# Steps with seven products in a float32 two-block decoder kernel: their number and place set per matrix pair, with buffers of their own

## The chip, the cores and the metric

The kernel runs on one core of one Trainium2 chip. The metric is device time in microseconds for one execution of the whole program. An execution is also taken with the hardware profiler; the traces below are of such executions, and their times (us) count from the first instruction.

## The reference, cut to what matters

Two decoder blocks on 256 tokens of width 2048, all in float32. Nearly all work is `activations (256 x 2048) @ weight (2048 x n)`:

```python
h = rms_norm(x, g)
(qa, ka, va, za, qb, kb, vb, zb, qm, zm, gates) = split(h @ w_in)      # 17408 columns
ya = moba_attention(rope(qa), rope(ka), va) * silu(za)
yb = dilated_mixture(rope(qb), rope(kb), vb) * silu(zb)
ym = memory_attention(qm, mem_n @ w_mem_kv) * silu(zm)
merged = g_a*(ya @ w_proj_a) + g_b*(yb @ w_proj_b) + g_m*(ym @ w_proj_m)
x1 = rms_norm(x + merged @ w_out, norm_final_g)
u = rmsnorm(x1, ln1_w)
lru_x, lru_g, q, k, v, ret_g = split(u @ w_in_2)                       # 6144 columns
y = concat(rg_lru(conv(lru_x)) * gelu(lru_g), retention(q, k, v, ret_g))
h1 = x1 + y @ w_out_2
u2 = rmsnorm(h1, ln2_w)
h2 = h1 + (silu(u2 @ w_ffn_gate) * (u2 @ w_ffn_up)) @ w_ffn_down       # 5632 wide
out = rmsnorm(h2, final_norm_w)
```

## The kernel before

**Splitting.** To reach float32 accuracy each operand is split in a rounded part and a rest (`hi`, `lo`; `split`, L327): ScalarE (ACT) copies to `hi`, VectorE (DVE) subtracts to get `lo`. A product of two 128x128 / 128x512 blocks is then three matmuls: hi·hi, hi·lo, lo·hi (L239 to L241, L179 to L181). The activations are split once (`Lhs`), the weights as they come: a 1 MB tile `raw` (three buffers) is loaded by SP's queue, and from it come `hi`/`lo` tiles of 128x2x512 (four buffers each).

**Single matrices** (`gemm`, L171): 512 output columns, two row tiles of 128 tokens, 16 blocks of 128 along the contraction. Each `hi`/`lo` tile feeds twelve matmuls.

**Pairs** (`pair_gemm`, L224): two matrices of 512 columns at once, in steps of 256 along the contraction. A step of kind "D" makes the plain eight block products (24 matmuls) from two `hi`/`lo` tiles. A step of kind "S" is Winograd's form of Strassen's scheme: seven products (21 matmuls), for which DVE first forms sums of weight blocks, `t13` (L274) and `t24` (L275, L276), and the activations' sums have been made once by `Lhs.put` (L160 to L169). It needs three full `hi`/`lo` tiles and a half one. The seven products go to PSUM banks "1" to "7", those of D steps to "2", "4", "3", "8". After the last S step (index `s1`) banks 1, 6, 7, 5 are combined (L294 to L298) and after the last step banks 2, 4, 3, 8 are added (L299 to L302), into four tiles `p1`, `vv`, `ww`, `yy` of the ring `w512` (eight buffers, L70).

**Which steps are S** stands in the table `STEPS` (L27), one string for each left operand: `lx` (first block's input), `u2` (input of gate/up), `ff` and `ff3` (input of the down matrix; `ff3` for the last three of the eleven 512-wide parts). The order of the steps is the order of the contraction. The matrices and their names in the traces: `qm`, `zm`, `qva`, `kza`, `gate` (three groups), `b` on `lx`; `wo` (both output matrices: `w_out` from L766, `w_out2` from L999); `lx`, `rq`, `rk`, `rv`, `lg`, `rg` (second block's input); `gu` (gate/up, L1037) and `fd` (down, L1054 and L1057). Before, the third gate group (`gate_one`, L644), both `wo` and all of the second block's input are single matrices.

**Side work** (attention, transposes for the next left operand, statistics) is cut into pieces that wait in two queues (`later`, `soon`); a `gemm` takes one up after each of its `hi`/`lo` tiles, a pair after each half of a D step that does not lie between its first and last S step (L290). `need` takes up pieces at once until a key is done.

**The order on each engine** is made by a scheduler from the program: it places instructions by its own estimate of time and gives a tile a buffer of its ring when one is free; each engine then runs its row in that order and waits on semaphores. 27 general buffers of 4 KB per partition (`slot`, L66) hold activations and results. The softmax tiles and `t13`, `t24` share two rings of two ("prob", "pt").

Of the kernel before, what the change touches and what calls it, by code (L numbers as in the profile page):

```python
# [13 lines left out]
ALU = mybir.AluOpType  # L14
# [37 lines left out]
def two_blocks(ctx: ExitStack, tc: tile.TileContext, x, xT, mem, memT, w_in, w_mem_kv, w_proj_a,  # L52
# [6 lines left out]
    sp = ctx.enter_context(tc.tile_pool(name="sp", bufs=NSLOT))  # L59
# [9 lines left out]
    def w512(name, shape=(P, 512)):  # L69
        return tp.tile(list(shape), F32, tag="w512", name=name, bufs=8)  # L70
# [52 lines left out]
    class Lhs:  # L123
# [24 lines left out]
        def put(self, i, src, gains=None, gain=None):  # L148
# [11 lines left out]
            a = tp.tile([P, 8, P], F32, tag="pt", name="fa")  # L160
# [10 lines left out]
    def gemm(name, w, r0, nk, col0, lhs, fine=False, tail=False, rate=1):  # L171
# [52 lines left out]
    def pair_gemm(name, wa, ca, wb, cb, lhs, r0=0):  # L224
        kinds = lhs.kinds
        n = len(kinds)
        s0, s1 = kinds.index("S"), kinds.rindex("S")
# [26 lines left out]
        for i, kind in enumerate(kinds):  # L254
            raw = wp.tile([P, 4, 512], F32, tag="raw", name="raw", bufs=3)
# [11 lines left out]
            if kind == "S":  # L267
# [35 lines left out]
        return (p1, w), (y, v)  # L303

# [183 lines left out]
    lx = load_T(xT, "gin", "hn", kinds=STEPS["lx"])  # L488
# [3 lines left out]
    for c, ps in enumerate(pair_gemm("qm", w_in, 9216, w_in, 9728, lx)):  # L492
# [3 lines left out]
    for ps in pair_gemm("zm", w_in, 10240, w_in, 10752, lx):  # L496
# [3 lines left out]
    def mem_attention(lhs, c):  # L500
# [4 lines left out]
        def scores(i):  # L505
# [10 lines left out]
            if i == 0:  # L516
                st["pr"] = tp.tile([P, 2, NT, S], F32, tag="prob", name="probm")
# [42 lines left out]
    for c in range(2):  # L560
        q, v = pair_gemm("qva", w_in, c * 512, w_in, 2048 + c * 512, lx)
        qa.append(evac_rope(q, tabs, "qaT"))
        va.append(evac_v(v, r_x, "va"))
        k, z = pair_gemm("kza", w_in, 1024 + c * 512, w_in, 3072 + c * 512, lx)
        ka.append(evac_rope(k, tabs, "kaT"))
        za.append(evac_silu(z, hr_x, "za"))
# [76 lines left out]

    def gate_one(gcol, c):  # L644
        ps = gemm("gate", w_in, 0, KD, 11264 + gcol * D + c * 512, lx)
        th = slot([P, NT, 512], "thg")
        for t in range(NT):
            A.activation(th[:, t], ps[t], AF.Tanh, scale=hr_x[:, t:t + 1])
        return th
# [33 lines left out]
    for one, two in (((0, 0), (2, 0)), ((1, 0), (2, 1)), ((0, 1), (2, 2)), ((1, 1), (3, 0)), ((0, 2), (1, 2))):  # L683
        for (n, g), ps in zip((one, two), pair_gemm("b", w_in, bcol(*one), w_in, bcol(*two), lx)):
# [4 lines left out]
    def dilated_attention(hi, lo, j, key):  # L689
        scale = 128.0 ** -0.5  # L690
        st = {}
        pts = [None, None]

        def scores(t):
# [44 lines left out]
        later(key, lambda: scores(0), lambda: turn(0, 1), lambda: scores(1), lambda: turn(1, 0),  # L739
# [7 lines left out]
    ths = [gate_one(1, c) for c in range(NCH)]  # L747
    mg = Lhs()
# [9 lines left out]
    lu = Lhs()  # L758
    ss1 = small([P, NT, NCH], "ss1", 1)
    ss2 = small([P, NT, NCH], "ss2", 1)  # L760
    for c in range(NCH):
# [4 lines left out]
        ps = gemm("wo", w_out, 0, KD, c * 512, mg)  # L766
# [125 lines left out]
    for c in range(2):  # L892
        ps = gemm("lx", w_in2, 0, KD, c * 512, lu)
# [240 lines left out]
```

## Time and profile before

| | us |
|---|---|
| time, median of 3 (lowest, highest) | 2211.64 (2208.92, 2212.5) |
| profiled execution, its own time | 2211.25 |
| its span, first to last instruction | 2209.5 |
| TensorE (PE) busy | 2174.9 (98%) |
| DVE busy | 1702.7 (77%) |
| ACT busy | 1167.6 (53%) |
| DMA, mean busy share of 16 engines | 57% |
| TensorE clock granted, mean over the span | 0.998 of full speed |

A matmul is shown with the time from its start to its modelled end, 0.39 us, while the next one starts 0.23 us later: so the busy time of PE is not read from the durations, but from how many matmuls stand in a stretch. An engine's idle time matters only where PE waits for it.

### The profile page before, as it was taken

What the parts mean: (1) busy time and instruction counts of PE and PEld (TensorE: products, weight loads), DVE (VectorE), ACT (ScalarE), POOL (GpSimd) and SP (SyncE); (2) the same over time, 40 slices, a digit from 0 to 9 for tenths busy, and PEclk for the clock granted to TensorE, in tenths of its full rate; (3) what the DMA queues carried; (4) which work ended last, traced back from release to release, by engine and by line L of the source; (5) the groups of instructions that cost most, each with busy time, mean ns of one, the idle gap of its engine ahead of it and who ended that gap; (6) DMA issues with size and microseconds to landing.
All of it is one profiled execution on the core that took longest, in us unless ns stands there. A gap on an engine that the chain in (4) does not pass through costs nothing.

```text
span 2209.5 us, 26102 instructions
## 1 busy us (share of the span) xinstructions
PE 2174.9 (98%) x9889; PEld 1790.1 (81%) x9889; DVE 1702.7 (77%) x2186; ACT 1167.6 (53%) x1452; POOL 9.2 (0%) x15
## 2 busy tenths in 40 slices
PE   8999999999999999999999999999999999999997
PEld 6888788788888888888888888888778888788776
DVE  5678778777678888556677777568998889988996
ACT  6755455555445555444554545555554555555553
POOL 0000000000000000000000000000000000000000
PEclk9999999999999999999999999999999999999999
DMA  8755465455565655446665545555555665565554
GB/s 305 250 187 191 144 208 174 172 171 190 191 210 175 220 196 178 158 149 215 213 212 184 177 153 173 188 172 191 191 190 192 207 202 182 191 211 188 191 196 147
DMA packets 219325, 421.80 MB, mean 191 GB/s; under 512 B 10816, under 2 KB 17088, under 8 KB 219200
## 3 DMA queue, kind: packets, MB, share of 16 engines
q1 hardware_dynamic: 218624, 419.09, 57.2%
q8 instruction: 77, 1.26, 0.2%
q10 hardware_dynamic: 576, 1.05, 0.1%
q14 instruction: 48, 0.39, 0.0%
HBM read 418.00 MB, written 2.10 MB: 190 GB/s over the span
## 4 chain that ended last, share of the span: by engine, by line
PE 86%; DVE 8%; DMA 3%; issue 1%; ACT 1%; SPq 0%; POOLq 0%; POOL 0%; ACTq 0%; DVEq 0%
PE gu L240 4%; PE gu L241 4%; PE gu L239 4%; DVE lo L330 3%; PE b L241 3%; PE b L240 3%; PE b L239 3%; PE wo L181 3%; PE wo L179 3%; PE wo L180 3%; PE gate L240 3%; PE gate L241 3%; PE gate L239 3%; PE fd L240 3%; PE fd L241 2%; PE fd L239 2%
## 5 line engine op out<-in xcount | busy, mean ns | idle before, releaser
L330 DVE TENSOR_TENSOR lo<-raw,hi 128x1024 fp32r<-128x1024 f32 x492 | 555.0, 1140 | 160.8 <-ACT hi L329 158.6
L329 ACT ACTIVATE hi<-raw 128x1024 fp32r<-128x1024 f32 x492 | 483.4, 995 | 369.0 <-PE gu L241 75.7
L201 DVE TENSOR_TENSOR lo<-raw,hi 128x1024 fp32r<-128x1024 f32 (+1 forms) x277 | 336.3, 1219 | 234.4 <-ACT hi L200 233.3
L200 ACT ACTIVATE hi<-raw 128x1024 fp32r<-128x1024 f32 (+1 forms) x277 | 291.9, 1056 | 349.8 <-PE wo L181 65.1
L329 ACT ACTIVATE hi<-t 128x1024 fp32r<-128x1024 f32 x146 | 154.5, 1058 | 177.3 <-DVE t L276 88.5
L330 DVE TENSOR_TENSOR lo<-t,hi 128x1024 fp32r<-128x1024 f32 x146 | 178.1, 1220 | 21.3 <-ACT hi L329 16.7
L274 DVE TENSOR_TENSOR t<-raw 128x1024 f32<-128x1024 f32 x73 | 89.0, 1220 | 26.0 <-DMA raw<-in_w_up_dram 15.5
L240 PE MATMUL gu<-lo,u20h 128*128 128x512 f32 x176 | 68.6, 390 | 0.0
L241 PE MATMUL gu<-hi,u20l 128*128 128x512 f32 x176 | 68.5, 389 | 0.0
L239 PE MATMUL gu<-hi,u20h 128*128 128x512 f32 x176 | 65.8, 395 | 0.0
L276 DVE TENSOR_TENSOR t<-t,raw 128x512 f32<-128x512 f32 x73 | 49.9, 684 | 0.3
L275 DVE TENSOR_TENSOR t<-t,raw 128x512 f32<-128x512 f32 x73 | 49.8, 683 | 0.1
L240 PE MATMUL gu<-lo,u22h 128*128 128x512 f32 x121 | 47.8, 395 | 1.3 <-DVE lo L330 1.1
L241 PE MATMUL gu<-hi,u21l 128*128 128x512 f32 x121 | 47.2, 390 | 0.0
L241 PE MATMUL gu<-hi,u22l 128*128 128x512 f32 x121 | 47.2, 390 | 0.0
L240 PE MATMUL gu<-lo,u21h 128*128 128x512 f32 x121 | 47.2, 390 | 0.0
L239 PE MATMUL gu<-hi,u22h 128*128 128x512 f32 x121 | 47.1, 389 | 0.0
L240 PE MATMUL gu<-lo,u23h 128*128 128x512 f32 x121 | 47.1, 389 | 0.0
L239 PE MATMUL gu<-hi,u23h 128*128 128x512 f32 x121 | 47.1, 389 | 0.0
L241 PE MATMUL gu<-hi,u23l 128*128 128x512 f32 x121 | 47.1, 389 | 0.0
L239 PE MATMUL gu<-hi,u21h 128*128 128x512 f32 x121 | 46.9, 399 | 0.0
L241 PEld LDWEIGHTS gu<-hi,u20l 128*128 128x128 f32 x176 | 33.0, 188 | 6.7
(1097 smaller groups left out, 5672.3 us busy)
## 6 DMA issues: line engine op xcount, KB each, us to landing
raw<-in_w_in_dram SPq DMA_DIRECT2D x240, 512.0 KB, 4.6
raw<-in_w_in_dram SPq DMA_DIRECT2D x64, 1024.0 KB, 5.2
raw<-in_w_gate_dram SPq DMA_DIRECT2D x88, 512.0 KB, 3.8
raw<-in_w_up_dram SPq DMA_DIRECT2D x88, 512.0 KB, 4.8
raw<-in_w_down_dram SPq DMA_DIRECT2D x76, 512.0 KB, 4.8
raw<-in_w_out_dram SPq DMA_DIRECT2D x32, 1024.0 KB, 5.1
raw<-in_w_mem_kv_dram SPq DMA_DIRECT2D x15, 1024.0 KB, 7.2
raw<-in_w_proj_m_dram SPq DMA_DIRECT2D x8, 1024.0 KB, 5.3
```

What stands on the lines that cost most here:

```text
L179: nc.tensor.matmul(ps[t], xh[:, c], hi, start=(kt == 0), stop=False)
L180: nc.tensor.matmul(ps[t], xh[:, c], lo, start=False, stop=False)
L181: nc.tensor.matmul(ps[t], xl[:, c], hi, start=False, stop=(kt == nk - 1))
L200: A.activation(hi[:, a:b], raw[:, h + a:h + b], AF.Copy)
L201: V.tensor_tensor(out=lo[:, a:b], in0=raw[:, h + a:h + b], in1=f32(hi[:, a:b]), op=ALU.subtract)
L239: nc.tensor.matmul(ps[b], xh, hi, start=first, stop=False)
L240: nc.tensor.matmul(ps[b], xh, lo, start=False, stop=False)
L241: nc.tensor.matmul(ps[b], xl, hi, start=False, stop=(left[b] == 0))
L274: V.tensor_tensor(out=t13, in0=raw[:, 2:3].to_broadcast([P, 2, 512]), in1=raw[:, 0::3], op=ALU.add)
L276: V.tensor_tensor(out=t24[:, 1], in0=t24[:, 0], in1=raw[:, 1], op=ALU.add)
L329: A.activation(hi, src, AF.Copy)
L330: V.tensor_tensor(out=lo, in0=src, in1=f32(hi), op=ALU.subtract)
```

## The change

The table `STEPS` becomes a table `CFG` with an entry for each left operand (which steps get sums) and for each pair (which of its steps are S). A pair may have fewer S steps than its left operand has sums; it takes the last ones, and the steps are done in an order of their own: the pair's string is followed, and each S takes the next contraction step with sums, each D the next without. The S steps of each use, for the whole program:

| pair | number of pairs | S per pair before | S per pair after |
|---|---|---|---|
| qm, zm | 2 | 2 (DDSSDDDD) | 3 (DDSDSDSD) |
| qva, kza, gate of memory, b | 11 | 2 (DDSSDDDD) | 2 (DDSDSDDD) |
| gate of causal attention | 2 | 2 (DDSSDDDD) | 3 (DDSDSDSD) |
| wo, first and second | 4 | single matrices, none | 2 (DDSDDSDD) |
| gu | 11 | 3 (DDSDSDSD) | 2 (DDSDDSDD) |
| fd, first eight parts | 4 | 2 (DDSDSDDD) | 2 (DDSDSDDD) |
| fd, last three parts | 1 | 2 (DDSDSD) | single matrices, none |

That is 73 S steps in 31 pairs before, and 72 in 34 pairs after. The other edits: within an S step `t24` is formed after the first `hi`/`lo` split, not before it; `t13`, `t24` and `fa` (the sums of `Lhs.put`) get a ring of their own with three buffers (`t4`); the softmax tiles take general buffers, which become 29; the ring `w512` shrinks from eight to six; in the dilated attention the second score piece comes before the first transposition.

```diff
-STEPS = {
-    "lx": "DDSSDDDD",
-    "u2": "DDSDSDSD",
-    "ff": "DDSDSDDD",
-    "ff3": "DDSDSD",
+CFG = {
+    "lx": "DDSDSDSD", "u2": "DDSDSDSD", "mg": "DDSDSDDD", "lu": "", "y2": "DDSDSDDD", "ff": "DDSDSDDD",
...
+    "gu": "DDSDDSDD", "fd": "DDSDSDDD",
 }
+SP = {"slot": 29, "w512": 6, "hl": 4, "t4": 3, "raw": 3}
...
-    def pair_gemm(name, wa, ca, wb, cb, lhs, r0=0):
-        kinds = lhs.kinds
+    def pair_gemm(name, wa, ca, wb, cb, lhs, r0=0, kinds=""):
+
         n = len(kinds)
+        with_sums = [i for i in range(n) if lhs.kinds[i] == "S"][-kinds.count("S"):]
+        without = [i for i in range(n) if i not in with_sums]
+        order = [(with_sums if kind == "S" else without).pop(0) for kind in kinds]
...
-                t13 = tp.tile([P, 2, 512], F32, tag="prob", name="t13")
-                t24 = tp.tile([P, 2, 512], F32, tag="pt", name="t24")
+                t13 = t4("t13", [P, 2, 512])
+                t24 = t4("t24", [P, 2, 512])
                 V.tensor_tensor(out=t13, in0=raw[:, 2:3].to_broadcast([P, 2, 512]), in1=raw[:, 0::3], op=ALU.add)
-                V.tensor_tensor(out=t24[:, 0], in0=t13[:, 0], in1=raw[:, 3], op=ALU.add)
-                V.tensor_tensor(out=t24[:, 1], in0=t24[:, 0], in1=raw[:, 1], op=ALU.add)
                 for src, banks in ((raw[:, 0:2], "12"), (t13, "57"), (t24, "64"), (raw[:, 3:4], "3")):
+                    if src is t13:
+                        V.tensor_tensor(out=t24[:, 0], in0=t13[:, 0], in1=raw[:, 3], op=ALU.add)
+                        V.tensor_tensor(out=t24[:, 1], in0=t24[:, 0], in1=raw[:, 1], op=ALU.add)
...
-        later(key, lambda: scores(0), lambda: turn(0, 1), lambda: scores(1), lambda: turn(1, 0),
+        later(key, lambda: scores(0), lambda: scores(1), lambda: turn(0, 1), lambda: turn(1, 0),
               lambda: turn(1, 1), values, finish)
...
-        ps = gemm("wo", w_out, 0, KD, c * 512, mg)
+        if c % 2 == 0:
+            both = two("wo", w_out, c * 512, w_out, c * 512 + 512, mg, "wo")
+        ps = next(both)
...
-            if final and c >= 2:
+            if final or "S" not in CFG["fd"]:
                 ps = gemm("fd", w_down, f0 * 512, 4 * nf, c * 512, ff, tail=(c == NCH - 1))
```

`two` is a small wrapper: with an "S" in the pair's string it calls `pair_gemm`, else two single `gemm`s.

Where the change moves instructions, the rows of DVE show it in three places (an L number is the line in the file of that kernel). The first is the middle of a gate/up pair. `t_...` are `t13` (128x1024) and `t24` (128x512), `lo<-raw,hi` and `lo<-t_...,hi` the splits. Before:

```order
L274 TENSOR_TENSOR t_12012<-raw 128x1024
L330 TENSOR_TENSOR lo<-raw,hi 128x512
L275 TENSOR_TENSOR t_12013<-t_12012,raw 128x512
L276 TENSOR_TENSOR t_12013<-t_12013,raw 128x512
L330 TENSOR_TENSOR lo<-raw,hi 128x1024 x3
L330 TENSOR_TENSOR lo<-t_12012,hi 128x1024
L330 TENSOR_TENSOR lo<-t_12013,hi 128x1024
L330 TENSOR_TENSOR lo<-raw,hi 128x512
```

After:

```order
L348 TENSOR_TENSOR lo<-raw,hi 128x512
L348 TENSOR_TENSOR lo<-raw,hi 128x1024 x4
L282 TENSOR_TENSOR t_12576<-raw 128x1024
L348 TENSOR_TENSOR lo<-raw,hi 128x1024
L285 TENSOR_TENSOR t_12577<-t_12576,raw 128x512
L286 TENSOR_TENSOR t_12577<-t_12577,raw 128x512
L348 TENSOR_TENSOR lo<-t_12576,hi 128x1024
L348 TENSOR_TENSOR lo<-t_12577,hi 128x1024
```

Before, the sums of the next S step begin before the last split of the one ahead (the 128x512 one), with the two splits of one D step behind; after, the four splits of two D steps stand between.

The second is the start of the last down matrices (`fd` of parts 8 to 10), from the end of the first pair's work on. `p_...`, `ww`, `yy`, `vv` are the pair's results, `x_...` the residual `h1`, `fwb` the final weights. Before:

```order
L1060 TENSOR_TENSOR x_8227<-x_8227,p_17246 128x512
L300 TENSOR_TENSOR ww<-fd_17032,ww 128x512
L301 TENSOR_TENSOR yy<-fd_17046,yy 128x512
L1065 TENSOR_TENSOR x_8227<-x_8227,fwb 128x512
L302 TENSOR_TENSOR vv<-fd_17050,vv 128x512
L1060 TENSOR_TENSOR x_8227<-x_8227,ww 128x512
L1060 TENSOR_TENSOR x_8402<-x_8402,yy 128x512
L1060 TENSOR_TENSOR x_8402<-x_8402,vv 128x512
L1065 TENSOR_TENSOR x_8227<-x_8227,fwb 128x512
L201 TENSOR_TENSOR lo<-raw,hi 128x1024
L1065 TENSOR_TENSOR x_8402<-x_8402,fwb 128x512 x2
L201 TENSOR_TENSOR lo<-raw,hi 128x1024 x8
```

After, the first two single matrices there (their results are read from the banks `fd`):

```order
L205 TENSOR_TENSOR lo<-raw,hi 128x1024 x2
L1080 TENSOR_TENSOR x_8476<-x_8476,fd 128x512 x2
L205 TENSOR_TENSOR lo<-raw,hi 128x1024
L1085 TENSOR_TENSOR x_8476<-x_8476,fwb 128x512 x2
L205 TENSOR_TENSOR lo<-raw,hi 128x1024 x5
L1080 TENSOR_TENSOR x_8485<-x_8485,fd 128x512 x2
L205 TENSOR_TENSOR lo<-raw,hi 128x1024
L1085 TENSOR_TENSOR x_8485<-x_8485,fwb 128x512 x2
```

Nine instructions on results stood ahead of the first split for the third matrix; after, no more than two stand between splits.

The third is the end of the second pair of the first output matrix, `wo`, where the second block's input matrices begin (`lo` of L205). `gfb` is the row of final-norm weights. Before, the end of the last two single matrices:

```order
L769 TENSOR_TENSOR x_8752<-wo,xres 128x512 x2
L201 TENSOR_TENSOR lo<-raw,hi 128x1024 x2
L333 SCALAR_TENSOR_TENSOR u3l<-trm,gg,u3h 128x256 x2
L775 TENSOR_TENSOR x_8752<-x_8752,gfb 128x512
L201 TENSOR_TENSOR lo<-raw,hi 128x1024
L333 SCALAR_TENSOR_TENSOR u3l<-trm,gg,u3h 128x256
L775 TENSOR_TENSOR x_8752<-x_8752,gfb 128x512
```

After:

```order
L205 TENSOR_TENSOR lo<-raw,hi 128x1024 x2
L308 TENSOR_TENSOR p_8768<-wo_8501,p_8768 128x512
L782 TENSOR_TENSOR x_8871<-p_8768,xres 128x512
L306 TENSOR_TENSOR yy<-wo_8627,vv 128x512
L205 TENSOR_TENSOR lo<-raw,hi 128x1024
L307 TENSOR_TENSOR vv<-wo_8627,ww 128x512
L310 TENSOR_TENSOR yy<-wo_8528,yy 128x512
L309 TENSOR_TENSOR ww<-wo_8505,ww 128x512
L311 TENSOR_TENSOR vv<-wo_8532,vv 128x512
L782 TENSOR_TENSOR x_8871<-ww,xres 128x512
L205 TENSOR_TENSOR lo<-raw,hi 128x1024
L788 TENSOR_TENSOR x_8476<-x_8476,gfb 128x512
```

In this pair L306 and L307, which need only S banks, stand behind L308, which needs the pair's last step; and the first multiplication by `gfb` (L788, for `x_8476`, the first of the four chunks) stands behind all of it, where before those of three chunks were done earlier.

## Rows read from the trace of the kernel before

**Rows 1.** The page's busy times, share of the span, instructions.
```profile
PE 2174.9 (98%) x9889; PEld 1790.1 (81%) x9889; DVE 1702.7 (77%) x2186; ACT 1167.6 (53%) x1452; POOL 9.2 (0%) x15
```

**Rows 2.** Waits of PE: who, for whom, us in total, times, longest.
```profile
PE gu L240 <- DVE lo L330: 4.2, 8, 1.2
PE fd L180 <- DVE lo L201: 3.9, 1, 3.9
PE gu L239 <- ACT hi L329: 2.7, 5, 0.6
PE trp L342 <- ACT probb L710: 1.7, 1, 1.7
PE gate L239 <- ACT hi L329: 1.5, 3, 0.9
PE kza L239 <- ACT hi L329: 1.0, 1, 1.0
```

**Rows 3.** Timeline of PE, last `fd`: start, duration, line, operation [idle before <- releaser].
```profile
2157.61 0.39 PE L239 MATMUL fd<-hi,ff10h 128*128 128x512 f32 x1
...
2161.69 0.61 PE L179 MATMUL fd<-hi,ff8h 128*128 128x512 f32 x2
2166.18 0.50 PE L180 MATMUL fd<-lo,ff8h 128*128 128x512 f32 x1 [3.87 <-DVE lo L201]
```

**Rows 4.** Part of the chain of waits: seven transposes of a gate/up result.
```profile
1785.35 0.76 PE trm L342 x7
```

**Rows 5.** Stretches: length, busy us (instructions) of engines, PEclk, DMA share, GB/s.
```profile
100.80:187.00 86.20, 86.20 (x390) 71.39 (x389) 64.94 (x77) 50.84 (x65) 0.70 (x1) 1.00 0.63 210
526.70:654.50 127.80, 127.80 (x565) 105.84 (x564) 91.60 (x98) 63.12 (x66) 0.00 (x0) 1.00 0.59 198
654.50:869.10 214.60, 214.60 (x964) 177.70 (x963) 177.19 (x209) 112.20 (x121) 0.00 (x0) 1.00 0.60 196
1006.90:1097.90 91.00, 91.00 (x419) 75.31 (x418) 55.44 (x64) 47.54 (x71) 0.00 (x0) 1.00 0.65 221
1387.10:1478.10 91.00, 91.00 (x418) 75.26 (x418) 55.54 (x67) 46.95 (x66) 0.00 (x0) 1.00 0.55 186
1478.10:1654.00 175.90, 172.25 (x766) 139.94 (x765) 158.55 (x195) 102.63 (x120) 0.69 (x1) 1.00 0.57 188
1654.00:1739.90 85.90, 85.76 (x382) 70.51 (x381) 72.34 (x82) 42.48 (x45) 0.00 (x0) 1.00 0.63 204
1739.90:1912.20 172.30, 170.47 (x758) 139.19 (x757) 157.79 (x186) 98.66 (x110) 0.00 (x0) 1.00 0.58 192
1997.90:2128.00 130.10, 128.42 (x566) 104.14 (x566) 116.67 (x136) 73.16 (x81) 0.00 (x0) 1.00 0.58 190
2128.00:2200.30 72.30, 67.66 (x291) 54.44 (x289) 55.84 (x72) 34.18 (x47) 0.55 (x1) 0.98 0.45 152
```

**Rows 6.** The same view, of the stretch behind the long wait of Rows 3.
```profile
2166.00:2172.00 6.00, 5.82 (x18) 4.66 (x19) 5.91 (x7) 1.06 (x1) 0.00 (x0) 0.72 0.40 116
```

**Rows 7.** Timeline of DVE at the end of a gate/up pair.
```profile
2123.41 0.68 DVE L296 TENSOR_TENSOR ww<-gu,vv 128x512 f32<-128x512 f32 x1
2124.01 0.68 DVE L297 TENSOR_TENSOR yy<-gu,vv 128x512 f32<-128x512 f32 x1
...
2131.36 2.35 DVE L330 TENSOR_TENSOR lo<-raw,hi 128x1024 fp32r<-128x1024 f32 x2
```

**Rows 8.** Timeline of ACT and DVE in `lx`: a square sum, then the factor `rr`.
```profile
1105.45 0.62 ACT L308 ACTIVATE junk<-x 128x512 f32<-128x512 f32 x1
...
1111.18 0.16 DVE L794 TENSOR_TENSOR rr<-r,r 128x2 f32<-128x2 f32 x1 [0.81 <-POOL r L793]
```

**Rows 9.** Costliest groups: the sums `t13`, one for each S step.
```profile
L274 DVE TENSOR_TENSOR t<-raw 128x1024 f32<-128x1024 f32 x73 | 89.0, 1220 | 26.0 <-DMA raw<-in_w_up_dram 15.5
```

More of the change, by code (lines that the diff above doesn't have):

```diff
@@ L253, in pair_gemm @@
         p1, v, w, y = [None] * 4
-        for i, kind in enumerate(kinds):
-            raw = wp.tile([P, 4, 512], F32, tag="raw", name="raw", bufs=3)
+        for n_, kind in enumerate(kinds):
+            i = order[n_]
+            raw = wp.tile([P, 4, 512], F32, tag="raw", name="raw", bufs=SP["raw"])
             for j, (wt, c) in enumerate(((wa, ca), (wb, cb))):
@@ L303, in pair_gemm, with two @@
         return (p1, w), (y, v)
+    def two(name, wa, ca, wb, cb, lhs, key):
+        kinds = CFG[key]
+        if "S" in kinds:
+            yield from pair_gemm(name, wa, ca, wb, cb, lhs, kinds=kinds)
+        else:
+            yield gemm(name, wa, 0, KD, ca, lhs)
+            yield gemm(name, wb, 0, KD, cb, lhs)
     def square_sum(src, acc):
@@ L495, in two_blocks @@
         evac_T(ps, r_x, qmT[c])
-    for ps in pair_gemm("zm", w_in, 10240, w_in, 10752, lx):
+    for ps in two("zm", w_in, 10240, w_in, 10752, lx, "zm"):
         zm.append(evac_silu(ps, hr_x, "zm"))
@@ L560, in two_blocks @@
     for c in range(2):
[L561 to L566, printed above, removed]
+        qv = two("qva", w_in, c * 512, w_in, 2048 + c * 512, lx, "qva")
+        qa.append(evac_rope(next(qv), tabs, "qaT"))
+        va.append(evac_v(next(qv), r_x, "va"))
+        kz = two("kza", w_in, 1024 + c * 512, w_in, 3072 + c * 512, lx, "kza")
+        ka.append(evac_rope(next(kz), tabs, "kaT"))
+        za.append(evac_silu(next(kz), hr_x, "za"))
     def causal_attention(hi, lo, c, hp, key):
@@ L642, in gate_pair @@
         return ths
[L644 to L649, printed above, removed]
     def project(c, th, w_proj, nk, lhs, first=False):
@@ L745, in two_blocks @@
         dilated_attention(hi, lo, j, key if j == 3 else None)
-    ths = [gate_one(1, c) for c in range(NCH)]
-    mg = Lhs()
+    ths = gate_pair(1, 0, "gb") + gate_pair(1, 2, "gb")
+    mg = Lhs(CFG["mg"])
     for c in range(NCH):
@@ L891, in two_blocks @@
     hl = []
-    for c in range(2):
-        ps = gemm("lx", w_in2, 0, KD, c * 512, lu)
+    for c, ps in enumerate(two("lx", w_in2, 0, w_in2, 512, lu, "l")):
         need("rr")
@@ L983, in gelu_branch @@
         later(key, pause, pause, lambda: piece(0), lambda: piece(1))
-    for c in range(2):
-        gelu_branch(c, gemm("lg", w_in2, 0, KD, 1024 + c * 512, lu))
-    for c in range(2):
-        sz = evac_silu(gemm("rg", w_in2, 0, KD, 5120 + c * 512, lu), hrr, "rsz")
+    for c, ps in enumerate(two("lg", w_in2, 1024, w_in2, 1536, lu, "l")):
+        gelu_branch(c, ps)
+    for c, ps in enumerate(two("rg", w_in2, 5120, w_in2, 5632, lu, "rg")):
+        sz = evac_silu(ps, hrr, "rsz")
         need(f"on{c}")
@@ L995, in two_blocks @@
     h1 = x1
-    lu2 = Lhs(STEPS["u2"])
+    lu2 = Lhs(CFG["u2"])
     ss3 = small([P, NT, NCH], "ss3", 1)
     for c in range(NCH):
-        ps = gemm("wo2", w_out2, 0, KD, c * 512, y2)
+        if c % 2 == 0:
+            both = two("wo2", w_out2, c * 512, w_out2, c * 512 + 512, y2, "wo2")
+        ps = next(both)
         for t in range(NT):
```

83 lines of the change are left out of this document (46 added, 37 removed).

## Prediction

> **What bounds the kernel now.** I read the page's first part, then PE's waits, then stretches. PE is 98% busy [rows 1], but a matmul's duration overlaps the next one's, so I count instead. In a dense stretch 18 matmuls start in 2161.69 - 2157.61 = 4.08 us, 0.2267 us each [rows 3]; a transpose takes 0.76 / 7 = 0.11 us [rows 4]. What a stage lasts beyond its matmuls and transposes (eight per pair, one pair late) is lost:
>
> - `b`, five pairs: 930 x 0.2267 + 3.5 = 214.3 of 214.6 us, lost 0.3, or 0.06 a pair; DVE busy 177.19 / 214.6 = 83% [rows 5].
> - `fd`, two pairs: 372 x 0.2267 + 0.9 = 85.2 of 85.9, lost 0.7, 0.35 a pair; DVE 84%.
> - `gu`, four, four and three pairs with 183 matmuls each: 169.4, 169.4 and 127.1 of 175.9, 172.3 and 130.1, lost 6.5, 2.9 and 3.0, together 12.4 or 0.7 to 1.6 a pair; DVE 90 to 92%.
> - `wo`, four single matrices, twice: 384 x 0.2267 + 3.5 = 90.6 of 91.0; DVE 61%.
> - the last `fd`: 282 x 0.2267 + 0.9 = 64.8 of 72.3, lost 7.5.
>
> So the kernel is bound by the number of matmuls, and in `gu` and the last `fd` DVE sets the pace on top. The waits say the same: `gu` waits for `lo` and `hi`, the last `fd` once 3.9 us for a `lo`, and in the first block `kza`, `gate` and a transposition `trp` (for the softmax on ACT) wait 4.2 us together [rows 2]. What to see: losses grow with DVE's share of the stage, not with PE's.
>
> **Terms, against the span of 2209.5 us.** Its own time was 2211.25, 1.75 above the span and 0.4 below the median of 2211.64.
>
> *Matmuls.* An S step has 21 instead of 24. The sums of S steps go from 73 [rows 9] to 72: 3 more matmuls x 0.2267 = **+0.7**. By place: +33 in `gu`, +6 in the last `fd`, -24 in the two `wo`, -12 in `qm`, `zm` and the second gate group.
>
> *What an S step costs DVE.* 512 columns take 0.60 us from start to start, and two splits of 1024 take 2.35, so the second adds 1.13 [rows 7]. Beyond a D step, S has t13 (1.13), t24 (2 x 0.60) and one and a half splits (1.13 + 0.60): 4.1 us, for 0.68 us less on PE. That is why the place counts.
>
> *gu.* Four pairs lose 4 x 4.1 us of DVE's 158.55 and gain 2.7 us of matmuls: 142 / 172 = 83%, the share of `b`. Per pair I take 0.2, between `b` (0.06) and `fd` (0.35): 11 x 0.2 = 2.2 instead of 12.4. The pairs' ends (four results, four products for `sg`) stay as they are; what covers them is the tiles split ahead, which now also has two D steps between two S steps, as the first order excerpt shows. New is the entry from the second `wo`: the third step of the first `gu` pair takes the fifth contraction step, whose activations are results of `wo`'s last pair. Adding up DVE's row from there to the split of t24 (sums and splits of two chunks, three weight splits, t13, t24) gives some 16 us, an estimate with the times above; PE arrives after 60 matmuls and 16 transposes, 15.3 us. I add 1.2 (0 to 3). Together 3.4 instead of 12.4: **-9.0**.
>
> *Last fd.* As single matrices it has no results to combine. The excerpt shows nine instructions ahead of the first split before and at most two between splits after; the wait of 3.9 us goes. So does its echo: behind it the granted clock was 0.72 for 6 us [rows 6], a mixture of the two levels 2.4 and 1.2 GHz. A single `gemm` with a light DVE is like `wo`, 0.4 for its four: **-7.0** (-7.5 to -5.9, if 1.6 as in a `gu` pair stays).
>
> *First block.* The two S steps in a row are taken apart, t24 comes behind a split, and `scores(1)` lies between `scores(0)` and its transposition. Of the 4.2 us I take three quarters: **-3.2** (-4.2 to 0).
>
> *Where S steps come in.* Each `wo` stage gets 4 x 4.1 us and 16 results of 0.60, 26 us on 55.5: 81.5 of 91.0 - 2.7 = 88.3, 92%; the first sheds six multiplications by `gfb` (3.6 us, third excerpt), 88%. That is `gu`'s range before, and I take its lower end, since some of the next operand's splits also move out: 4 pairs x 0.7 = +2.8 (1.4 to 6.4). `qm` and `zm` rise from 75 to 86%, the second gate group from 72 to 79% [rows 5]: 0.2 for each of four pairs, +0.8 (0 to 1.4). In `lx` the factor `rr` comes late: before 13.3 us after the stage began at 1097.9 [rows 8]. Now the statistics of three chunks more stand ahead, 12 square sums of 0.62 on ACT with six multiplications of 0.60 between them, so 24 us, up to 28 with weight splits between. After two copies of 0.7 PE's transposition `trc` takes it; it stands behind 116 matmuls and 16 transposes, at 28 us. Loss 0 to 1.4, taken 0.7. Sum **+4.3**.
>
> DMA moves the same bytes; wo's 1 MB loads become two of 512 KB on the same queue, at a share of 0.55 to 0.65 [rows 5]: nothing, unless `raw` is released late.
>
> Total: 0.7 - 9.0 - 7.0 - 3.2 + 4.3 = -14.2, a span of 2195.3, and with the 1.75 around it **2197.0 us**, 0.7% less.
>
> **A rule against it.** Two 1024-wide splits follow at 1.13, not at their full 1.22 [rows 7, 9], and 512-wide ones at 0.60, not at 0.68. The Trainium skill (VectorE: DVE Perf Modes, "The TRN2 errata") prices a float32 tensor_tensor at (N+151)/0.96 ns, that is 0.69 and 1.22 us each, and says in "The DRAIN you can't avoid" that the next operation starts only when the pipe is empty. By that, as an estimate, an S step would cost 4.5 us and `wo` would reach about 95% on DVE; its pairs would then lose at least what `gu`'s worst do, 6.4 instead of 2.8, and the time would be 2200.6. The durations agree with the page, the distances in the trace do not, and I follow the distances.
>
> **Rivals.**
>
> 1. *gu's waits come from the pair's end and the ring of three `raw`, not from the S steps.* For: all `gu` pairs share a sequence of results, `sg` products and splits, and most of its waits are short (8 in 4.2 us, 5 in 2.7 [rows 2]) and come back. Against: `b` and `fd` have the same results and ring and lose little. Then `gu` keeps 12.4 (+9.0) and the new `wo` pairs lose `gu`'s mean of 1.1 (+1.7): 2207.7, 0.18% less. The Trainium skill (Perfetto Trace Analysis, "Optimization Strategy") reads bubbles that repeat as a sign of too few buffers; by that rule this rival is right. The recurring gaps fit it, the nearly gapless `b` with the same buffers does not.
> 2. *Slower: `w512` with six buffers.* In `wo`'s second pair the third excerpt shows L306 and L307 behind L308, because three buffers hold `gfb` rows. If results slip so on the chip in each of the 11 `gu` pairs, which hold four results and two `th`, three DVE operations of 0.60 lie bare at every end: 11 x 1.8 = 19.8, 2216.8. It decides once DVE has less than 1.8 us split ahead at a pair's end. Against: in that row of DVE the slip stands in this one pair only, and buffers of `gu`'s ring have a whole pair's time to come free.
> 3. *Nothing new is lost.* Without the remainders (3.4 in `gu`, 0.5 in `fd`, 1.0 in the first block, 4.3 new): 2187.8. For: four tiles ahead cover nearly 11 us in D steps, and `b` shows that 83% costs nothing. Against: `wo` gets past that.
> 4. *It only moves waits about.* PE's work is the same to three matmuls; if the S steps lose elsewhere what they lost in `gu`, the time stays at 2212. Against: `wo` has 35 us of DVE to spare in 91, `gu` 17 in 176 [rows 5].
>
> **How the numbers follow.** Forecast 0.60; rivals 1 to 4: 0.14, 0.07, 0.13, 0.06. A measurement tells a difference from about 0.2%, 4.4 us, so faster means below 2207.2. Rival 1 lies on that line and is halved. Faster: 0.60 + 0.13 + 0.07 = 0.80; same: 0.07 + 0.06 = 0.13; slower 0.07. The range goes from rival 3 to rival 1, 2187.5 to 2208, which leaves out rivals 2 and 4 and some of 3's edge.
>
> **What would show it.** Right: `gu` stages of about 173, 173 and 129 us with single gaps; the last `fd` at 67 without a wait over 1 us and at full clock; both `wo` near 89; no long `trp` wait. Wrong: `gu` as long as before plus 2.7 (rival 1); DVE's final results behind PE's end in each `gu` pair (rival 2); waits of PE for `lo` in `wo` of more than 1.6 us a pair, a stop at `trc` in `lx` of over 2 us, or one in the first `gu` pair of over 3.

## The result and the profile after

| | before | after |
|---|---|---|
| median, us (lowest to highest) | 2211.1 (2208.92 to 2212.5) | 2189.93 (2188.3 to 2190.89) |
| span of the profiled run, us | 2209.5 | 2186.5 |

The ratio is 0.9904, interval 0.9887 to 0.9922: 21 us less. The forecast was 2197.0, range 2187.5 to 2208; the sign and the range held, the fall is 7 us larger than forecast. The profiled execution after, 2188.3, is the fastest of its four, so the spans, and the stages below, differ by 23 us.

The page's busy times of the kernel after, against [rows 1], and the chain of work that ended last, by engine, before and then after:

```profile
PE 2165.1 (99%) x9892; PEld 1791.3 (82%) x9892; DVE 1716.4 (79%) x2218; ACT 1174.6 (54%) x1459; POOL 9.2 (0%) x15
...
PE 86%; DVE 8%; DMA 3%; issue 1%; ACT 1%; SPq 0%; POOLq 0%; POOL 0%; ACTq 0%; DVEq 0%
...
PE 95%; DVE 2%; DMA 1%; ACT 1%; issue 1%; SPq 0%; POOL 0%; POOLq 0%; DVEq 0%; ACTq 0%
```

DVE does more than before in a shorter span, and still PE waits less. Its waits after, against [rows 2] (who, for whom, us in total, times, longest); the one of `mk` at the start was there before (6.1):

```profile
PE mk L183 <- ACT mn0h L350: 6.0, 1, 6.0
...
PE gu L246 <- ACT hi L347: 1.0, 1, 1.0
PE wo L246 <- ACT hi L347: 1.0, 1, 1.0
PE qm L247 <- DVE lo L348: 0.6, 1, 0.6
PE trc L360 <- ACT ev L854: 0.4, 1, 0.4
```

The wait of 3.9 us in the last `fd`, the recurring ones of `gu` and the one of `trp` for `probb` are gone. Stretches of after, columns as in [rows 5]; in order: `qva`/`kza`, gate of memory, third gate, `wo`, start of `lx`, second `wo`, three times `gu`, last `fd`.

```profile
186.10:375.60 189.50, 189.50 (x866) 157.15 (x865) 154.50 (x199) 99.28 (x123) 0.00 (x0) 1.00 0.55 180
375.60:520.90 145.30, 145.12 (x694) 120.41 (x693) 111.11 (x171) 76.95 (x114) 0.00 (x0) 1.00 0.52 174
862.00:972.70 110.70, 110.70 (x589) 93.69 (x588) 63.88 (x95) 51.40 (x74) 0.00 (x0) 1.00 0.47 158
997.40:1085.00 87.60, 87.60 (x399) 72.15 (x398) 73.99 (x90) 46.14 (x54) 0.00 (x0) 1.00 0.68 224
1085.00:1180.10 95.10, 94.73 (x434) 77.99 (x433) 77.23 (x120) 58.72 (x96) 1.39 (x2) 1.00 0.62 204
1375.60:1464.70 89.10, 87.87 (x397) 72.03 (x396) 73.52 (x91) 50.66 (x66) 0.00 (x0) 1.00 0.57 189
1464.70:1640.10 175.40, 174.18 (x785) 143.41 (x784) 150.72 (x188) 100.95 (x122) 0.70 (x1) 1.00 0.57 192
1725.40:1896.90 171.50, 171.50 (x769) 142.01 (x768) 144.35 (x168) 93.18 (x102) 0.00 (x0) 1.00 0.59 196
1982.20:2110.60 128.40, 128.40 (x575) 106.32 (x574) 106.16 (x118) 67.86 (x73) 0.00 (x0) 1.00 0.59 197
2110.60:2177.00 66.40, 66.40 (x297) 54.65 (x295) 39.93 (x47) 29.00 (x39) 0.55 (x1) 1.00 0.46 158
```

The first three were, before:

```profile
187.00:378.70 191.70, 190.20 (x865) 156.81 (x864) 153.38 (x197) 97.99 (x122) 0.00 (x0) 1.00 0.53 176
378.70:526.70 148.00, 146.22 (x694) 120.26 (x694) 111.60 (x171) 76.69 (x114) 0.00 (x0) 1.00 0.51 171
869.10:982.30 113.20, 111.31 (x590) 93.38 (x588) 63.62 (x95) 51.92 (x74) 0.00 (x0) 1.00 0.45 154
```

Stage by stage, matmuls included, with what the terms of the prediction come to:

| stage | forecast, us | measured, us |
|---|---|---|
| `qm`, `zm`, second gate group | -1.9 | -1.8 |
| rest of the first block: `qva` to the gate of memory; third gate | -3.2 | -4.9; -2.5 |
| both `wo` | -2.6 | -5.3 |
| `lx` to `rg` | +0.7 | +1.4 |
| `gu` | -1.5 | -3.0 |
| first two `fd` | 0 | -1.0 |
| last `fd` | -5.6 | -5.9 |
| sum | -14.1 (-14.2 before rounding) | -23.0 |

### The profile page after: what moved, and what is told of

It reads as the page before. It is cut to its first block, busy times and chain, and to the rows that moved or that the text cites. A ratio compares the mean times of both kernels' runs of the same rounds, so it can differ in the third digit from the quotient of the medians.

```text
span 2186.5 us, 26210 instructions
## 1 busy us (share of the span) xinstructions
PE 2165.1 (99%) x9892; PEld 1791.3 (82%) x9892; DVE 1716.4 (79%) x2218; ACT 1174.6 (54%) x1459; POOL 9.2 (0%) x15
## 4 chain that ended last, share of the span: by engine, by line
PE 95%; DVE 2%; DMA 1%; ACT 1%; issue 1%; SPq 0%; POOL 0%; POOLq 0%; DVEq 0%; ACTq 0%
PE gu L247 7%; PE gu L248 7%; PE gu L246 7%; PE b L248 3%; PE b L246 3%; PE b L247 3%; PE gate L246 3%; PE fd L248 3%; PE fd L247 3%; PE fd L246 3%; PE gate L248 3%; PE gate L247 3%; PE wo L247 3%; PE wo L248 2%; PE wo L246 2%; PE proj L185 2%
## 5 line engine op out<-in xcount | busy, mean ns | idle before, releaser
L347 ACT ACTIVATE hi<-raw 128x1024 fp32r<-128x1024 f32 (+1 forms) x544 | 540.4, 1003 | 444.7 <-PE gu L248 114.8
L348 DVE TENSOR_TENSOR lo<-raw,hi 128x1024 fp32r<-128x1024 f32 (+1 forms) x544 | 619.4, 1151 | 169.0 <-ACT hi L347 164.0
L205 DVE TENSOR_TENSOR lo<-raw,hi 128x1024 fp32r<-128x1024 f32 (+1 forms) x225 | 272.5, 1219 | 167.5 <-ACT hi L204 166.8
L204 ACT ACTIVATE hi<-raw 128x1024 fp32r<-128x1024 f32 (+1 forms) x225 | 236.6, 1055 | 279.1 <-PE rqk L185 42.1
L246 PE MATMUL gu<-hi,u20h 128*128 128x512 f32 x176 | 70.4, 400 | 0.0
L248 PE MATMUL gu<-hi,u21l 128*128 128x512 f32 x176 | 68.5, 389 | 0.0
L247 PE MATMUL gu<-lo,u21h 128*128 128x512 f32 x176 | 68.5, 389 | 0.0
L246 PE MATMUL gu<-hi,u21h 128*128 128x512 f32 x176 | 68.3, 389 | 0.0
```

The lines of the kernel that those rows point to most:

```text
L204: A.activation(hi[:, a:b], raw[:, h + a:h + b], AF.Copy)
L205: V.tensor_tensor(out=lo[:, a:b], in0=raw[:, h + a:h + b], in1=f32(hi[:, a:b]), op=ALU.subtract)
L246: nc.tensor.matmul(ps[b], xh, hi, start=first, stop=False)
L247: nc.tensor.matmul(ps[b], xh, lo, start=False, stop=False)
L248: nc.tensor.matmul(ps[b], xl, hi, start=False, stop=(left[b] == 0))
L347: A.activation(hi, src, AF.Copy)
```

## The experiments

All are the kernel after with the edit shown; times are medians. In one stage the same code took different times: `qm` 41.9 to 45.0 us in the runs with three `raw`. So totals within 2 us of each other don't decide, and stages are compared.

**Three S steps in gate/up again**, then the same with four `raw`:

```diff
-    "gu": "DDSDDSDD", "fd": "DDSDSDDD",
+    "gu": "DDSDSDSD", "fd": "DDSDSDDD",
```

> The kernel after with three S steps per gate/up pair again (33 matmuls less, 7.5 us of PE), all else as after: the new rings, t24 behind the first split and the other pairs stay. Theory D (the losses of gate/up come from DVE's share): the gate/up stages go back towards 175.9, 172.3 and 130.1 us, so about 3 us over those of after, 2193 us; DVE about 91% there and PE's waits for lo and hi in gu back at some 5 to 7 us. Between, if the third buffer for the sums and the later t24 had a part: 2187. Rival 1 (pair end and ring of three raw): the losses are not tied to S steps, so the stages shorten by the matmuls alone, to about 169, 169 and 126 us, and the time is 2181.

```diff
-SP = {"slot": 29, "w512": 6, "hl": 4, "t4": 3, "raw": 3}
+SP = {"slot": 27, "w512": 6, "hl": 4, "t4": 3, "raw": 4}
```

> As the run before (three S steps per gate/up pair), with four buffers of raw instead of three, paid by two general buffers. Rival 1 (too few buffers for the loads): the waits of gu vanish, and the time is some 7 us under that of after, 2182. Theory D (DVE's work): within 1.5 us of the run with three buffers, about 2193, with DVE still over 90% busy in gate/up.

Measured: 2194.96 with three `raw`, 2187.59 with four. The first is what theory D said, the second refutes that DVE's work alone explains it. The third `gu` stage, first with three `raw`, then with four (columns as in [rows 5]):

```profile
1987.40:2116.90 129.50, 127.97 (x566) 104.28 (x565) 114.65 (x131) 71.60 (x79) 0.00 (x0) 1.00 0.58 191
```

```profile
1983.20:2109.60 126.40, 126.40 (x566) 104.51 (x565) 113.85 (x129) 71.91 (x79) 0.00 (x0) 1.00 0.60 197
```

DVE is busy for 114 us in both, so the share is higher where nothing is lost: 113.85 / 126.4 = 90% against 114.65 / 129.5 = 89%. Waits of DVE in these two stretches, three `raw` ahead of four:

```profile
DVE lo L348 <- ACT hi L347: 9.5, 10, 1.2
DVE t L282 <- DMA raw<-in_w_up_dram: 5.2, 5, 1.4
```

```profile
DVE lo L348 <- ACT hi L347: 11.5, 12, 1.1
```

With three buffers, t13 of the next S step waits for its load, DVE stands still, and that time is missing at the splits. The first two stages gain less by the fourth buffer, 0.7 and 1.3 us against 3.1 in the third, and had less of this wait with three (0.8 and 3.1 against 5.2). The scheduler also orders DVE's row in another way when it has a fourth buffer; how much of the gain is that order was not told apart. The kernel before had the wait in the same stage, and the kernel after, with two S steps, has none there; first before, then after, waits of DVE in the third `gu` stage:

```profile
DVE t L274 <- DMA raw<-in_w_up_dram: 5.6, 6, 1.8
```

```profile
DVE lo L348 <- ACT hi L347: 20.4, 23, 1.5
...
```

So in this stage either edit removes that wait: fewer S steps or a fourth buffer. In the first two stages after still has 4.0 us of it, and with two S steps no pair but the one at the entry is longer for it. By the code, an S step's `raw` is read last by the fourth split, a D step's by the second. What four buffers leave in the first two `gu` stages (176.7 and 171.8) is 4.0 us at the entry (below), in the first two pairs, and 1.4 us in each of the third and fourth pairs. DVE there, from a pair's results on (four `raw`, second `gu` stage):

```profile
1815.70 0.69 DVE L171 TENSOR_TENSOR fa<-fa 128x128 f32<-128x128 f32 x3
...
1816.90 0.29 DVE L171 TENSOR_TENSOR fa<-fa 128x128 f32<-128x128 f32 x1
...
1818.84 0.69 DVE L348 TENSOR_TENSOR ff5x<-fa,ff5x 128x512 fp32r<-128x512 f32 x1
1819.44 1.22 DVE L282 TENSOR_TENSOR t<-raw 128x1024 f32<-128x1024 f32 x1
```

and PE at the first S step behind it:

```profile
1825.34 0.50 PE L246 MATMUL gu<-hi,u21x 128*128 128x512 f32 x1 [0.53 <-ACT hi L347]
```

The chunk just finished gets sums for an S step of `fd`: four of 0.2 us and one split of 0.60, 1.4 us ahead of t13. The third `gu` stage needs no such sums and loses nothing.

**A version from this**: four `raw`, the second `wo` single, three S steps only in the six pairs without such sums ahead and not at the entry (its lines on `raw` and `wo` are not shown).

```diff
-    "gu": "DDSDDSDD", "fd": "DDSDSDDD",
+    "gu": "DDSDDSDD", "gu3": "DDSDSDSD", "fd": "DDSDSDDD",
...
-            pg, pu = two("gu", w_gate, f * 512, w_up, f * 512, lu2, "gu")
+            pg, pu = two("gu", w_gate, f * 512, w_up, f * 512, lu2, "gu" if f in (0, 2, 3, 6, 7) else "gu3")
```

> A version meant to beat both: four buffers of raw (27 general buffers), the second output matrix single again, and in gate/up three S steps in the six pairs whose preceding results need no sums for the down matrix, two in the other five. From the run with three S steps and four raw (2187.6): in the pairs that follow a chunk with sums DVE has four sums and two splits more between a pair's end and the first S step, and PE lost about 1.3 us there, five times. Theory: against after 18 matmuls less in gate/up (-4.1), the second output matrix +1.8, the entry to gate/up -2.9, third gate/up stage and the rest as they were: 2184.7. Rival (four raw buffers bring nothing of their own, the three-S pairs lose 0.7 us each as in the run with three raw): 2189.

Measured: 2185.39. The theory holds; some 1.5 us stay in the third pair of each of the first two parts (44.6 and 44.7 us, where its neighbours with two S steps take 43.1). Next, those two pairs as DDDSDSDD, and `b` with three S steps (the second pair of lines), shown against this mixed version:

```diff
-    "gu": "DDSDDSDD", "gu3": "DDSDSDSD", "fd": "DDSDSDDD",
+    "gu": "DDSDDSDD", "gu3": "DDSDSDSD", "gul": "DDDSDSDD", "fd": "DDSDSDDD",
...
-    "gb": "", "b": "DDSDSDDD", "wo": "DDSDDSDD", "l": "", "rv": "", "rg": "", "rqk": "", "wo2": "",
+    "gb": "", "b": "DDSDSDSD", "wo": "DDSDDSDD", "l": "", "rv": "", "rg": "", "rqk": "", "wo2": "",
...
-            pg, pu = two("gu", w_gate, f * 512, w_up, f * 512, lu2, "gu" if f in (0, 2, 3, 6, 7) else "gu3")
+            pg, pu = two("gu", w_gate, f * 512, w_up, f * 512, lu2, "gul" if f in (2, 6) else "gu" if f in (0, 3, 7) else "gu3")
```

> The mixed version with two more edits: the five pairs b with three S steps (15 matmuls less, 3.4 us; DVE there from about 83 to 93%), and the two gate/up pairs in which PE still lost 1.2 us at their first S step with that step one D step later (DDDSDSDD). Theory with four raw buffers (93% of DVE costs little where no other work stands between a pair's end and the first S step): b from 214.6 to 212, gate/up 2.4 us less, 2180.4. Rival (DVE's share sets the loss whatever the buffers): b loses 0.7 to 1 us a pair and stays at 214.6 or more, 2183.

Measured: 2197.33; two edits of opposite sign. `gu` gains 1.9 (172.8 and 170.4), `b` with the third gate loses 13. Five pairs `b`:

```profile
646.30:870.30 224.00, 214.56 (x948) 175.47 (x947) 194.64 (x228) 120.77 (x131) 0.00 (x0) 0.99 0.56 188
```

and PE's waits that are new in this kernel:

```profile
PE trq L360 <- DVE ra L465: 5.6, 3, 1.9
PE b L247 <- DVE lo L348: 3.8, 4, 1.8
PE gate L184 <- DVE lo L205: 1.8, 1, 1.8
```

Here PE's transposition waits for the rotary products `ra`, which DVE makes from the pair's results: a third S step puts one D step instead of three behind the last S step. Both theories were too kind; whether the share or that place decides here wasn't told apart. Without the edit on `b` (its lines of the diff left out):

> The mixed version (2185.4 us) with one edit more: in the two gate/up pairs in which PE still lost 1.2 us at their first S step (the third pair of each of the first two parts) the steps are DDDSDSDD, so that this S step comes one D step later behind the pair's end; the pairs b stay at two S steps. Theory (DVE, late by four sums and two splits there, has caught up by then): the first two gate/up stages go from 173.3 and 171.8 to about 172.8 and 170.4, all else is as in the mixed version, 2183.5 us. Rival (the two S steps, now only one D step apart, lose it again at the second): 2185.4 or more.

Measured: 2183.21, ratio to before 0.9874 (0.9857 to 0.9890), the fastest here, with no wait of PE in `gu`; its first two `gu` stages:

```profile
1466.20:1638.20 172.00, 172.00 (x775) 142.26 (x774) 150.29 (x183) 98.99 (x114) 0.69 (x1) 1.00 0.59 194
1723.50:1893.80 170.30, 170.30 (x763) 140.83 (x762) 151.23 (x177) 96.23 (x106) 0.00 (x0) 1.00 0.60 196
```

**Both output matrices single again**

```diff
-    "lx": "DDSDSDSD", "u2": "DDSDSDSD", "mg": "DDSDSDDD", "lu": "", "y2": "DDSDSDDD", "ff": "DDSDSDDD",
+    "lx": "DDSDSDSD", "u2": "DDSDSDSD", "mg": "", "lu": "", "y2": "", "ff": "DDSDSDDD",
...
-    "gb": "", "b": "DDSDSDDD", "wo": "DDSDDSDD", "l": "", "rv": "", "rg": "", "rqk": "", "wo2": "DDSDDSDD",
+    "gb": "", "b": "DDSDSDDD", "wo": "", "l": "", "rv": "", "rg": "", "rqk": "", "wo2": "",
```

> Both output matrices as single matrices again, all else as after. 24 matmuls more, 5.4 us. Theory D: both wo stages at 91.0 us, which is 5.3 us more than after; in return the wait at the first gate/up step (1.6 us, its third step needs results of the last wo pair) and the late factor in lx (about 1 us) go: 2192.5 us. Rival: the wait at the entry to gate/up belongs to the order of its own steps, and lx is longer for another reason; then nothing comes back and the time is 2195.

Measured: 2189.68, no different from after. The two `wo` give up 5.3 us, and more comes back than expected: `lx` 1.6 (the first line, its first three matrices), the first `gu` stage 2.9 (the second):

```profile
1089.30:1182.80 93.50, 93.50 (x426) 77.42 (x425) 69.48 (x104) 50.28 (x68) 1.39 (x2) 1.00 0.61 199
...
1469.20:1641.70 172.50, 172.50 (x777) 142.79 (x776) 145.92 (x177) 97.12 (x112) 0.69 (x1) 1.00 0.58 193
```

In the kernel after, PE stops in the first `gu` pair's first S step:

```profile
1481.40 0.50 PE L246 MATMUL gu<-hi,u22x 128*128 128x512 f32 x1 [0.99 <-ACT hi L347]
```

Not all that comes back was lost. With a pair, the last two chunks are done together, and eight transpositions of `x` move from each `wo` into the stage behind it. The instructions on the transposed tiles `trm` in the first `gu` stage, before and then after (PE first, POOL left out; with single `wo` there are 32 again):

```profile
1478.10:1654.00 175.90, 4.78 (x32) 3.87 (x32) 3.60 (x6) 5.00 (x10) 1.00 0.57 188
1464.70:1640.10 175.40, 5.98 (x40) 4.96 (x40) 4.68 (x8) 7.10 (x14) 1.00 0.57 192
```

At 0.11 us each [rows 4] that is 0.9 us; so 0.7 in `lx` and 2.0 at the entry are losses. Together -0.8, where the prediction's own terms give -5.4 + 2.8 + 0.7 + 1.2 = -0.7. This part of the change is worth nothing.

**The last down matrices with a pair again**

```diff
-        ff = Lhs("" if final else CFG["ff"])
+        ff = Lhs("DDSDSD" if final else CFG["ff"])
...
-            if final or "S" not in CFG["fd"]:
+            if final and c >= 2:
...
-                                     kinds=CFG["fd"])
+                                     kinds="DDSDSD" if final else CFG["fd"])
```

> The first two column blocks of the last down matrices as a pair with two S steps again (6 matmuls less, 1.4 us), all else as after. Theory D (the pair's results stand ahead of the first split for the third matrix on DVE): the last stage goes from 66.4 to some 72 us with one wait of PE for lo of 3 to 4 us and a lower granted clock behind it, 2195.5 us. Rival (the wait came from the shared rings of the sums and of the results, which are other rings now): the stage shortens by its matmuls to 65 us, 2188.5.

Measured: 2194.99, the stage 71.8 us. The same wait as in [rows 3] is back, and matmuls 0.43 us apart follow it (timeline of PE):

```profile
2150.38 0.80 PE L184 MATMUL fd<-lo,ff8h 128*128 128x512 f32 x1 [3.87 <-DVE lo L205]
...
2152.68 0.63 PE L184 MATMUL fd<-lo,ff8h 128*128 128x512 f32 x1
2153.11 0.63 PE L185 MATMUL fd<-hi,ff8l 128*128 128x512 f32 x1
```

The stretch behind the wait (columns as in [rows 5]):

```profile
2150.40:2156.40 6.00, 6.00 (x15) 4.75 (x16) 4.75 (x6) 1.06 (x1) 0.00 (x0) 0.54 0.40 134
```

Theory D as expected; the rings are those of after here, so the rival falls.

**What took the first block's waits away.** Four runs. S steps in a row again in `qva`, `kza` and the gate of memory:

```diff
-    "qm": "DDSDSDSD", "zm": "DDSDSDSD", "qva": "DDSDSDDD", "kza": "DDSDSDDD", "gm": "DDSDSDDD", "ga": "DDSDSDSD",
+    "qm": "DDSDSDSD", "zm": "DDSDSDSD", "qva": "DDSSDDDD", "kza": "DDSSDDDD", "gm": "DDSSDDDD", "ga": "DDSDSDSD",
```

> The kernel after with the two S steps in a row again (DDSSDDDD) in the pairs qva, kza and the gate of memory, six pairs; all else as after. The stretch of these pairs (qva to the projection behind the gate of memory) was 339.8 us before and 334.8 after. Theory (steps in a row leave DVE no D step to get ahead): it goes back to about 339.5, and the time rises by 4.7 us to 2194.6. Rival (the sums' own ring and the later t24 took the waits away): the stretch stays within 1 us of 334.8, 2190.

Measured: 2190.12, that stretch 334.8 us as in after. The theory falls. The sums t13 and t24 in rings shared with the softmax tiles again:

```diff
-                t13 = t4("t13", [P, 2, 512])
-                t24 = t4("t24", [P, 2, 512])
+                t13 = tp.tile([P, 2, 512], F32, tag="prob", name="t13")
+                t24 = tp.tile([P, 2, 512], F32, tag="pt", name="t24")
...
```

> The kernel after with t13 in one ring of two with the softmax rows, and t24 and fa in another with their transposed copies, as before the change (28 general buffers); all other edits stay. The stretch qva to the projection behind the gate of memory was 339.8 us before and 334.8 after, and neither taking the S steps apart nor the place of t24 made that difference. Theory (there the softmax tiles hold the sums' buffers, so that S steps wait): the stretch goes back towards 339 us, and the time to some 2194. Rival (something else, such as the number of general buffers): 335 us and 2190.

Measured: the stretch 337.5, 2.7 of the 4.9 us back. So with the sums' own ring all 4.9 us come even with steps in a row. Without it 2.2 are left; whether steps apart do that or the other edits that this run shares with after (t24's place, the buffer counts) is not shown. A wait of DVE in this stretch of before shows the sharing (t13 waits until PE has transposed the softmax tile):

```profile
DVE t L274 <- PE trp L342: 1.9, 1, 1.9
```

The total stays (2189.43), because the second `wo` with the first `gu` stage takes 87.4 + 173.7 us, not 89.1 + 175.4. Two rings of two are four buffers where after has three, and t13 no longer shares its ring with `fa` and t24: t13 of the first S step of that `gu` stage starts 5.0 us behind the stage's first matmul, in after 8.9 (DVE, this run and then after), and no wait of PE in these two stages is listed any more.

```profile
1473.85 1.22 DVE L282 TENSOR_TENSOR t<-raw 128x1024 f32<-128x1024 f32 x1
...
1473.60 1.21 DVE L282 TENSOR_TENSOR t<-raw 128x1024 f32<-128x1024 f32 x1
```

It is not the one general buffer less: the run with eight `w512` below has as many, and there the two stages take 89.1 and 175.4. With t24 ahead of the first split:

```diff
+                V.tensor_tensor(out=t24[:, 0], in0=t13[:, 0], in1=raw[:, 3], op=ALU.add)
+                V.tensor_tensor(out=t24[:, 1], in0=t24[:, 0], in1=raw[:, 1], op=ALU.add)
                 for src, banks in ((raw[:, 0:2], "12"), (t13, "57"), (t24, "64"), (raw[:, 3:4], "3")):
-                    if src is t13:
-                        V.tensor_tensor(out=t24[:, 0], in0=t13[:, 0], in1=raw[:, 3], op=ALU.add)
-                        V.tensor_tensor(out=t24[:, 1], in0=t24[:, 0], in1=raw[:, 1], op=ALU.add)
```

> The kernel after with t24 formed before the first split of an S step again, all else as after. The first split of each of the 72 S steps then comes 1.2 us later on DVE. If the four tiles split ahead cover that (gate/up now at 83% of DVE): gate/up stages within 0.5 us of 175.4, 171.5 and 128.4, 2190.5. If the later t24 had carried part of the gain: 0.2 to 0.4 us lost at each S step of the denser stages (gate/up, both output matrices, the first block), 5 to 12 us more, 2195 to 2202.

Measured: 2190.36, all `gu` stages as in after: the place of t24 does nothing, with the sums' own ring. The dilated attention's old order:

```diff
-        later(key, lambda: scores(0), lambda: scores(1), lambda: turn(0, 1), lambda: turn(1, 0),
+        later(key, lambda: scores(0), lambda: turn(0, 1), lambda: scores(1), lambda: turn(1, 0),
```

> The kernel after with the dilated attention's pieces in the old order (first transposition before the second scores), all else as after. The third gate stage, in which these pieces run, was 113.2 us before and 110.7 after. Theory (the first transposition comes before ACT has its softmax done): the wait of PE for probb of 1.7 us is back, that stage at 113 us, the time at 2192.4. Rival (the softmax tiles' own buffers took the wait away): 110.7 and 2190.

Measured: 2193.46, the third gate stage 115.2 us, so the order is worth 4.5 there, more than the 2.5 by which the stage got shorter; why it is 2.0 longer here than before the change was not traced. The wait is back:

```profile
PE trp L360 <- ACT probb L721: 2.1, 1, 2.1
```

**Eight `w512`**

```diff
-SP = {"slot": 29, "w512": 6, "hl": 4, "t4": 3, "raw": 3}
+SP = {"slot": 28, "w512": 8, "hl": 4, "t4": 3, "raw": 3}
```

> The kernel after with eight buffers w512 instead of six, paid by one general buffer (28). Theory (in the second pair of the first output matrix the rows gfb hold three of six, so that results slip and the factor rr comes late): lx, 95.1 us for its first three matrices against 93.5 with single output matrices, goes down to 93.5 to 94, the time to 2188.5. Rival 2 (results slip in gate/up for want of these buffers): the gate/up stages shorten too, by up to 20 us in all. If the number of statistics alone makes rr late: 95.1 and 2190.

Measured: 2190.65; `lx` 94.5 instead of 95.1, `gu` unchanged at 175.4, 171.5 and 128.4. Rival 2 falls. PE's wait for `trc` (0.4 in the list of after) is gone, and what `lx` still has over the 93.5 with single `wo` is the eight transpositions, 0.9: so the late `rr` is a matter of these buffers.

## Why the prediction was right, and where it was not

- **Matmuls and the last `fd`: right.** 66.4 us forecast as 67, granted clock 1.00; the run with a pair brings wait and clock back, so the step (the pair's results ahead of a split) is shown.
- **`gu`: the amount nearly right, the reason half.** The prediction counts 32, 32 and 24 transpositions in the three stages; the traces have 32, 24 and 16 before, and 40, 24 and 16 after. So 14.0 us were lost before, not 12.4, and 2.7 after (2.3, 0.2 and 0.2), forecast 3.4: 11.3 came back, not 9.0. But I wrote that DVE's share sets the loss. Between three and four `raw` the share says nothing. Counted in the same way, three S steps lose 14.9 us with three `raw` and 9.8 with four: 5.1 hang on that ring; of the rest 4.0 stand at the entry and 5.8 in the pairs behind the sums for `fd`. A share near 90% costs when DVE also stands still for a load or has extra work between a pair's end and an S step. [rows 9] said so: in the row that I read for a count, 15.5 us of DVE's idle time stood against loads of `w_up`. Rival 1 was dismissed because `b` has the same ring and no gaps; `b` has two S steps, and in `gu` it is three S steps with three `raw` that lose. (With three S steps `b` takes 224.0 us even with four `raw`, so the ring is not all there is to it.) Its forecast (12.4 kept) was wrong, its cause partly right. The Trainium skill (Perfetto Trace Analysis, "Optimization Strategy") says that repeating gaps can mean too few buffers; the run with four `raw` agrees for 5.1 of the 14.9 us.
- **The entry to `gu`: mis-sized.** 1.2 forecast, 2.0 found (2.9 less the 0.9 of the transpositions), of which 0.99 is PE's listed wait. The prediction added up DVE's row but not that t13 shares a ring of three with `fa` and t24; with two rings of two, 1.7 of the 2.0 are gone.
- **`wo`: mis-sized.** Loss taken as 2.8, found as 1.9: the stages are 5.3 us shorter, and by the 24 matmuls and 16 transpositions that left them it would be 7.2. Of the 1.9, 1.7 stand in the second and go with two rings of two. DVE was busy 73.99 / 87.6 = 84% and 73.52 / 89.1 = 83%, not 88 and 92: the stages got 18.5 and 18.0 us more of DVE, not 22.4 and 26. In the first, four of the sixteen results run behind its end, and four splits of the next operand moved out. The rule of the Trainium skill weighed there (VectorE: DVE Perf Modes, "The DRAIN you can't avoid") would, as the prediction used it, have had 95% and 6.4 us, further off. The same paragraph goes on that a next operation which is not held starts earlier; the prediction did not weigh that, so, unlike what it says, the starts 0.60 and 1.13 us apart [rows 7] do not speak against the page. `lx` came as forecast (0.7), `wo` lost less and the entry more, so the net of -0.7 came out right by errors that cancel.
- **First block: the largest miss**, -7.4 for -3.2. The listed waits (4.2) count only idle time behind a matmul's modelled end, and I did not set these stages' lengths against their matmuls. Of the three causes I named, steps in a row and t24 were not needed; the order of the scores was (4.5), and so was one that I did not name, the sums' own ring (2.7 at least).
- **First two `fd`**, -1.0, were forecast at nothing although 0.7 was listed as lost there. They take 86.0 and 86.3 us again with three S steps in `gu`, and 85.3 each with four `raw` besides, as in after; so the ring of loads has a part here too.

The time came out 2 us above rival 3, but not by its mechanism: losses remain at the entry, in the second `wo` and in `lx`, and the first block, which gave 7.4 us where 4.2 were listed, pays for them. Rival 4 falls with the result.

## What to carry over

A high busy share of a helper engine is not a bound by itself: look at what it waits for (here loads into a ring of three, and sums that share one) and at what stands between the last result and the next tile that the main engine needs. Saved matmuls in one stage can come back as late operands at the next stage's entry, so judge an edit over the stages behind it too. Lost time is read from stage lengths less counted work, not from the list of waits alone; and the work is counted in each trace anew, because small pieces (here eight transpositions) move between stages.

## What was not expected of the hardware

- `qm` at the start took 42.4 us after and 41.9 to 45.0 in the experiments with three `raw`, with the same row of DVE in all but the one that moves t24; in the longest, t13 waited for a load by up to 3.2 us. It took 41.5 in all four with four `raw`, where DVE's row also has a t13 earlier; so whether the buffer or that order takes the variation away is not shown.
- After 3.87 us without work the clock was granted at 0.54 over the next 6 us (matmuls 0.43 us apart, the 1.2 GHz level) in one run and at 0.72 in before; behind the 1 us waits of `gu` and `wo` matmuls kept 0.23 us.
